# A hybrid trunk layer on one core: KT transposed behind the scores, an opening between the joins, and a merge that begins in the front

## The chip, the cores and the metric

The kernel runs on one core of a Trainium2 chip. The metric is the device time in microseconds, the median over runs. Besides the runs there is one profiled execution of each kernel, from which all rows and durations below come.

## The reference, cut to what matters

One layer: a norm, one wide projection, an RWKV-7 branch (8 heads of 64), a forgetting-attention branch (8 heads), a gated merge of both, an output product, and an MLP. There are 512 tokens and 16 meta tokens ahead of them (T = 528), D_MODEL = 1024, D_FF = 4096, all in float32.

```python
def reference(x, meta, norm_mix, w_in, b_gate, ..., w_out_rw, w_out_fx, w_o, norm_mlp, w_up, w_down):
    h = jnp.concatenate([meta_b, x], axis=1)
    u = rmsnorm(h, norm_mix[l])
    proj = u @ w_in[l]
    feat_rw = proj[..., :C_RW]
    feat_fx = proj[..., C_RW:C_RW + C_FX]
    gates = jax.nn.sigmoid((proj[..., C_RW + C_FX:] + b_gate[l]).astype(jnp.float32))
    y_rw = rwkv7_branch(feat_rw, ...)     # S_t = S_{t-1} (diag(w_t) + a_t^T b_t) + v_t^T k_t ;  y_t = S_t r_t
    y_fx = fox_branch(feat_fx, ...)       # softmax(q k^T * scale + F_q - F_k) v, causal
    merged = gates[..., :D_MODEL] * (y_rw @ w_out_rw[l]) + gates[..., D_MODEL:] * (y_fx @ w_out_fx[l])
    h = h + merged @ w_o[l]
    z = rmsnorm(h, norm_mlp[l])
    h = h + jnp.square(jax.nn.relu(z @ w_up[l])) @ w_down[l]
    return h[:, N_META:]
```

## The kernel before

**Products.** A weight block of 128 x 512 comes by DMA as `wraw`; ScalarE (ACT) casts it to `whi`, VectorE (DVE) subtracts for the low part `wlo`. The activations are split in the same way, and each product is three matmuls: high by high, high by low and low by high (`passes`). The projections write tiles `pj` (L582), 24 matmuls of 264 columns for half of a block of 128 features.

**The front.** Up to 400 us, the order of TensorE (PE) is written out by `Turns`: streams of work, each a generator that yields a function saying when it can go on. The stream of the lowest rank that is ready, by the estimate in `Clock`, issues its next piece. Ranks: 0 the chains, 1 the recurrent part (decay, keys, scores, inverse), 2 attention, 3 its features, 4 group norm and the split of the branch outputs, 8 the projections, which fill what is left. `Clock.read` books every new instruction on its engine with an estimated duration. Only PE is held to this order; the other engines' queues are ordered by the scheduler, with priority for ranks 0 and 1. An instruction waits in its engine's queue until all it reads is there, and what is behind it waits with it.

**PSUM.** Eight banks: four under the tag "sm" (scores, transposes, attention), two "pj" for projections, one "ch" and one "py" for the chain, which the projections borrow when no chain runs. A ring gives a bank back when its reader is done.

**Scores** (`scores`, L951). A pair is two heads. Its nine chunks go in three groups. A group takes two sm banks: `sb` is read by DVE into `Bm` (L965), `sk` by DVE into two halves of `L` (L967). Then the three chunks of `KT` are transposed into a third bank, `pbt` (L971), which ACT copies to `bkT`. `KT` (L924) is made by DVE from `BK` (L922).

**Inverse and chain.** `inverse` joins the halves of a triangular inverse with small matmuls (32 x 32 and 64 x 32 tiles). The chain then goes chunk by chunk: `Rs` (L1111) is the copy that its second matmul needs. L893 is the scan `lc` of a pair's decay. `nm` (L762) is a maximum of attention, `y_rw` (L1095) the chain's output.

**Merge** (L1250 to L1273). For each of eight blocks m and both branches, four k-blocks by three passes go into a bank "sm" (`po`, L1267); DVE multiplies it with the gate `gl` (L1269), a tile that is loaded from DRAM (`gd`, stored by L596), and passed through tanh on ACT (L1262) first. The tiles `gl` lie where tiles of the front lay. ACT has another function table for tanh than for the front's exp and ln, hence a table load there. Then come the output product (L1298, L1329) and the MLP (L1357, L1484).

Of the kernel before, what the change touches and what calls it, by code (L numbers as in the profile page):

```python
# [62 lines left out]
class Clock:  # L63
# [35 lines left out]
    def read(self):  # L99

        new = self.nc.cur_bb.bb.instructions[self.seen:]
        self.seen += len(new)
        for x in new:
            outs = [o.bass_ap for o in x.outs if hasattr(o, "bass_ap")]
            ins = [o.bass_ap for o in x.ins if hasattr(o, "bass_ap")]
            if not outs:
                continue
            for o in outs:
                t = o.tensor
                if hasattr(t, "cap_key") and t.name not in self.free:  # L110
                    ring, n = self.rings.setdefault(str(t.cap_key).rsplit("_", 2)[0], []), t.tag_meta.bufs
                    self.free[t.name] = self.last(ring[-n]) if len(ring) >= n else 0.0
                    ring.append(t.name)
            names = [a.tensor.name for a in ins]
            out = outs[0].tensor.name
            eng = "Pool" if out.startswith("wlo") else str(x.engine).split(".")[-1]

            def cols(a):
                return math.prod(n for _, n in a.ap[1:])
            deps = max([self.w.get(n, 0.0) for n in names] + [self.free.get(out, 0.0)])  # L120
            if eng == "PE":
                n = cols(outs[0])
                rows, width = x.tile_size
                if ins[0].dtype == F32R:
                    cost = n / 2400 + 0.013
                else:
                    cost = n / 600 * max(rows * width / 16384, 1 / 4)
                if self.form != tuple(x.tile_size):
                    self.form = tuple(x.tile_size)
                    cost += 0.1  # L130
                self.pe = end = max(self.pe, deps) + cost
            else:
                size = max([cols(a) for a in outs + (ins if "Reduce" in str(x.opcode) else [])])
                if eng in self.RATE and "DMA" not in str(x.opcode):
                    fixed, per = self.RATE[eng]
                    if eng == "DVE" and (getattr(x, "is_tensor_tensor_scan", False) or any(a.ap[-1][0] > 4 for a in outs + (ins[:1] if "Transpose" in str(x.opcode) else []))):
                        per *= 2
                    end = self.book(eng, max(deps, self.last(out)), fixed + per * size) + fixed + per * size
                else:
                    cost = 0.3 + size * 128 * 4 / 2.0e5  # L140
                    end = self.book("DMA", max(deps, self.last(out)), cost) + cost + 2.0
            for o in outs:
                self.w[o.tensor.name] = max(self.w.get(o.tensor.name, 0.0), end + self.HOP)
            for n in names:
                self.r[n] = max(self.r.get(n, 0.0), end + self.HOP)
# [44 lines left out]
def kernel(ctx, tc, ht, x, win, par, cst, gain, lora, wout, wo, wup, wdn, out, dbg=None):  # L190
# [92 lines left out]
    ps = ctx.enter_context(tc.tile_pool(name="ps", bufs=2, space=PSUM))  # L283
    gates_d = [dr.tile([128, S], F32, name=f"gd{i}") for i in range(16)]
    ys = {}
    quarters = [[wdn[i][256 * c:256 * c + 256] for c in range(8)] for i in range(4)]

    with ExitStack() as st:
# [254 lines left out]
        def convert(job, raws):  # L543
# [9 lines left out]
                w.append((hi, lo))  # L553
            return job, w

        def projections(total):
            fetched, done = None, 0
            while done < total:
                if fetched is None:
                    yield lambda: 0.0 if jobs else math.inf  # L560
                    fetched = fetch(jobs.pop(0))
                cur = convert(*fetched)
                fetched = fetch(jobs.pop(0)) if jobs else None
                while cur is not None:
                    (_, _, _, begin, parts, ev, need), w = cur
                    nxt = convert(*fetched) if fetched else None
                    fetched = fetch(jobs.pop(0)) if jobs else None
                    if need is not None:
                        yield need
                    evac = begin()  # L570
                    for a0, a1 in parts:
                        po = None
                        n = 0
                        for k in range(KB):
                            if k % 2 == 0 or a1 - a0 > 300:
                                yield lambda f=po is None: max(ck.ready(*w[k // 4]), block_bank()[0] if f else 0.0)
                            if po is None:
                                tag = block_bank()[2]
                                po = ppj(tag)[:, :a1 - a0]
                                lent.extend([tag] * (tag != "pj"))  # L580
                            for a, b in passes(wk(w, k), U):
                                mm(po, a, b[:, k, a0:a1], start=n == 0, stop=n == 23)  # L582
                                n += 1
                        evac(po, slice(a0, a1))
                        if tag in lent:
                            lent.remove(tag)
                    ev.done = True
                    done += 1
                    cur = nxt

        def gate_job(i):
            def begin():
# [13 lines left out]
        def two(j, k):  # L606
            ys[4 * j + k] = t = kp.tile([128, 2, S], F32R, name="ys", tag=SLOTS[(4 * j + k) // 2], bufs=2)
            return t[:, 0, :], t[:, 1, :]

        def divided():  # L610
            yield chained[1]
            for k in range(2):
                split(*two(0, k), y_rw[:, k, :])
            for k in range(3):
                yield fox_done[k]
                split(*two(1, k), y_fx[:, k, :])
            yield normalised[1][1]
            for k in range(2, 4):
                split(*two(0, k), y_rw[:, k, :])

        forgot = Event()

# [102 lines left out]
        def attention():  # L725
# [3 lines left out]
            for p in range(4):  # L729
# [67 lines left out]
                def mixed():  # L797
# [10 lines left out]
                    if p < 3:  # L808
                        A.copy(y_fx[:, p, :], py)
                    else:  # L810
                        yield chained[1]
                        split(*two(1, 3), py)

                pes = yield from scored(0)
                for i in range(4):
# [39 lines left out]
        class Pair:  # L855
# [96 lines left out]
            def scores(self):  # L952
# [5 lines left out]
                for c0 in range(0, NCH, 3):  # L958
# [6 lines left out]
                    V.tensor_tensor(Bm[:, c0:c0 + 3, :], sb[:, :3, :], bc(tmask, 1, 3), ALU.mult)  # L965
                    for e, os in enumerate(hss[::-1]):
                        V.tensor_tensor(L[e][os, c0:c0 + 3, :], sk[os, :3, :], bc(tmask[os], 1, 3), ALU.mult)  # L967
                    yield lambda: max(ck.ready(KT) + 1.0, banks(1))
                    pb = psm("pbt").rearrange("p (a b) -> p a b", b=128)
                    for c in range(c0, c0 + 3):  # L970
                        nc.tensor.transpose(pb[:, c - c0, :], KT[:, c, :, :].rearrange("p a b -> p (a b)"), ident)  # L971
# [4 lines left out]
        def inverse(g, Bms, late):  # L976
# [54 lines left out]
            for n, pr_, c in cells:  # L1031
                for e, hs in enumerate(hss):
                    mm(p1[hs, n, :], Tt[qs[2 * e], c, pr_, :], W2[qs[2 * e], n, :], start=True, stop=True)
            for n, pr_, c in cells:
                for q in range(4):
                    mm(p2[qs[q], n, :], W2[qs[q], n, :], Tt[qs[q], c, pr_, half(q)], start=True, stop=True)
# [190 lines left out]
        turns.add(3, fox_features())  # L1227
        turns.add(4, divided())
        turns.add(8, projections(24 + 16))
        for i in range(16):  # L1230
            ask(9, B_GATE + i, gate_job(i), SEQ)
        with tc.manual_schedule(engines={mybir.EngineType.PE}):
# [16 lines left out]

    with ExitStack() as st:  # L1250
        mp = st.enter_context(tc.tile_pool(name="mp", bufs=1))
        ahead = [load_w(wout[0])]
        mhi = mp.tile([128, KB, S], F32R, name="mhi")
        mlo = mp.tile([128, KB, S], F32R, name="mlo")
        table["pin"] = None
        for m in range(KB):
            w = ahead.pop() if ahead else load_w(wout[m])
            pp = []
            for br in range(2):
                g = mp.tile([128, S], F32, name=f"gl{br}", bufs=2)  # L1260
                nc.sync.dma_start(g, gates_d[8 * br + m])
                act(g, g, AF.Tanh, scale=0.5)  # L1262
                po = ppo()
                n = 0
                for k in range(4 * br, 4 * br + 4):
                    for a, b in passes(wk(w, k), (0, 1)):
                        mm(po, a, ys[k][:, b, :], start=n == 0, stop=n == 11)  # L1267
                        n += 1
                V.scalar_tensor_tensor(g, g, 1.0, po, ALU.add, ALU.mult)  # L1269
                pp.append(g)  # L1270
# [20 lines left out]

        pd = [ppo(), ppo(), ppd(), ppd()]
        for b2 in range(4):
            w = load_w(wo[0, b2])
            for i, b1 in [(i, b1) for b1 in range(2) for i in range(4)] if b2 < 3 else [(i, b1) for i in range(4) for b1 in range(2)]:
                k = 2 * b2 + b1
                for n, (a, b) in enumerate(passes(M, w[b1])):
                    mm(pd[i], a[:, k, 128 * i:128 * i + 128], b, start=k == 0 and n == 0, stop=k == 7 and n == 2)  # L1298
# [317 lines left out]
```

## Time and profile before

| | us |
|---|---|
| median of 3 runs | 828.11 (827.68 to 828.64) |
| profiled execution | 826.71 |
| its span | 824.9 |
| PE busy | 808.1 |
| DVE busy | 607.8 |
| ACT busy | 452.5 |
| GpSimd busy | 120.0 |

PE is the engine that is always busy; the granted clock is 0.998 of 2.4 GHz in the mean. Records of PE overlap, so a matmul's cost is taken from the start of one to the start of the next. Stages by PE's lines: the norm up to 31 us, the front to 400, the merge to 445, the output product to 491, the MLP to the end.

### The profile page before, as it was taken

The page shows a single profiled execution, that of the slowest core. Times are in us where ns is not written, and L with a number is a line of the kernel's source. Part 1 is how long each engine was busy: PE and PEld are TensorE (multiplying, and loading weights), DVE is VectorE, ACT ScalarE, POOL GpSimd, SP SyncE. Part 2 cuts the span into 40 slices and gives each one's busy share as a digit, 9 for nine tenths or more (in the row PEclk, how much of TensorE's full clock was granted, in tenths as well). Part 3 has the DMA queues.
Part 4 walks back from the last instruction along what each step waited for, and adds up shares of the span by engine and source line. Part 5 has one row for each costly group of instructions (what it writes and reads, how often), then busy time and mean ns, then how long its engine had stood idle before and what let it go on. Part 6 is the DMA issues. An engine that isn't in the chain of part 4 may idle for free.

```text
span 824.9 us, 15506 instructions
## 1 busy us (share of the span) xinstructions
PE 808.1 (98%) x5886; PEld 667.3 (81%) x5886; DVE 607.8 (74%) x1196; ACT 452.5 (55%) x941; POOL 120.0 (15%) x124
## 2 busy tenths in 40 slices
PE   8999999998999999999999999999999999999998
PEld 6979887876987886778788889888888888888886
DVE  6797985687779855975267655875698678867988
ACT  7767548766575457664366534664445434543452
POOL 1021000010011000000022003100740174017400
PEclk9999999999999999999999999999999999999999
DMA  7222221211211311223687404533742365236532
GB/s 240 75 71 79 69 92 56 79 40 65 79 52 54 128 46 61 90 66 116 218 289 226 159 0 151 176 82 100 225 150 87 115 221 150 77 118 208 156 107 76
DMA packets 51483, 95.88 MB, mean 116 GB/s; under 512 B 5832, under 2 KB 7240, under 8 KB 51408
## 3 DMA queue, kind: packets, MB, share of 16 engines
q1 hardware_dynamic: 47680, 86.37, 33.0%
q0 software_dynamic: 1280, 4.20, 1.7%
q10 hardware_dynamic: 2448, 4.33, 1.5%
q8 instruction: 46, 0.75, 0.4%
q14 instruction: 29, 0.24, 0.1%
HBM read 88.56 MB, written 6.31 MB: 115 GB/s over the span
## 4 chain that ended last, share of the span: by engine, by line
PE 86%; DVE 5%; ACT 5%; issue 2%; DMA 1%; POOL 0%; DVEq 0%; ACTq 0%; SPq 0%
PE pj L582 22%; PE po L1357 21%; PE po L1484 12%; PE pd L1484 5%; PE po L1267 4%; PE po L1329 3%; PE pj L394 1%; PE pd L1298 1%; PE po L1298 1%; PE psc L751 1%; PE py L805 1%; PE psr L964 1%; PE ppt L788 1%; DVE wlo L551 1%; PE pch L1115 1%
## 5 line engine op out<-in xcount | busy, mean ns | idle before, releaser
L582 PE MATMUL pj<-uhi,whi 128*128 128x264 f32 (+1 forms) x480 | 164.3, 342 | 0.0
L582 PE MATMUL pj<-uhi,wlo 128*128 128x264 f32 (+1 forms) x480 | 153.9, 321 | 1.8 <-DVE wlo L551 1.8
L582 PE MATMUL pj<-ulo,whi 128*128 128x264 f32 (+1 forms) x480 | 153.8, 320 | 0.0
L242 DVE TENSOR_TENSOR wlo<-wraw,whi 128x512 fp32r<-128x512 f32 x84 | 81.0, 973 | 36.8 <-ACT whi L242 36.8
L582 PEld LDWEIGHTS pj<-uhi,whi 128*128 128x128 f32 x480 | 90.7, 189 | 12.9 <-issue 4.4
L582 PEld LDWEIGHTS pj<-uhi,wlo 128*128 128x128 f32 x480 | 90.7, 189 | 8.8 <-DVE wlo L551 2.2
L582 PEld LDWEIGHTS pj<-ulo,whi 128*128 128x128 f32 x480 | 91.0, 190 | 6.7 <-issue 1.6
L1357 PE MATMUL po<-zhi,whi 128*128 128x512 f32 (+1 forms) x248 | 94.8, 382 | 0.0
L1357 PE MATMUL po<-zlo,whi 128*128 128x512 f32 (+1 forms) x248 | 94.8, 382 | 0.0
L1357 PE MATMUL po<-zhi,wlo 128*128 128x512 f32 (+1 forms) x248 | 94.8, 382 | 0.0
L242 ACT CAST whi<-wraw 128x512 fp32r<-128x512 f32 x84 | 51.4, 617 | 53.5 <-PE po L1357 20.3
L551 DVE TENSOR_TENSOR wlo<-wraw,whi 128x512 fp32r<-128x512 f32 x78 | 53.8, 699 | 23.5 <-ACT whi L550 22.6
L550 ACT CAST whi<-wraw 128x512 fp32r<-128x512 f32 x78 | 47.7, 617 | 42.4 <-PE pj L582 41.7
L276 ACT CAST whi<-t 128x512 fp32r<-128x512 f32 x64 | 39.9, 624 | 44.6 <-DVE wlo L276 27.2
L1406 POOL TENSOR_TENSOR t<-traw 128x512 f32<-128x512 f32 x24 | 38.4, 1622 | 173.6 <-DMA traw<-in_wdn 173.6
L1484 PE MATMUL po<-wlo,fhi 128*128 128x512 f32 (+1 forms) x164 | 63.4, 387 | 0.2
L1484 PE MATMUL po<-whi,flo 128*128 128x512 f32 (+1 forms) x164 | 62.8, 384 | 0.0
L1484 PE MATMUL po<-whi,fhi 128*128 128x512 f32 (+1 forms) x164 | 62.3, 384 | 0.0
L276 DVE TENSOR_TENSOR wlo<-t,whi 128x512 fp32r<-128x512 f32 x64 | 43.5, 689 | 24.3 <-ACT whi L276 24.0
L1373 ACT CAST fhi<-R 128x768 fp32r<-128x768 f32 (+1 forms) x32 | 30.2, 945 | 49.1 <-DVE R L1380 26.1
L1357 PEld LDWEIGHTS po<-zlo,whi 128*128 128x128 f32 x248 | 46.6, 188 | 9.1
L1357 PEld LDWEIGHTS po<-zhi,wlo 128*128 128x128 f32 x248 | 46.6, 188 | 9.0
(330 smaller groups left out, 1706.4 us busy)
## 6 DMA issues: line engine op xcount, KB each, us to landing
wraw<-in_win SPq DMA_DIRECT2D x84, 256.0 KB, 2.6
wraw<-in_wup SPq DMA_DIRECT2D x60, 256.0 KB, 3.1
wraw<-in_wdn SPq DMA_DIRECT2D x48, 256.0 KB, 2.7
traw<-in_wdn SPq DMA_DIRECT2D x48, 256.0 KB, 3.5
gd<-gt ACTq DMA_DIRECT2D x16, 256.0 KB, 2.2
wraw<-in_wout SPq DMA_DIRECT2D x16, 256.0 KB, 3.9
gl<-gd SPq DMA_DIRECT2D x16, 256.0 KB, 3.8
traw<-in_wdn POOLq DMA_DIRECT2D x16, 256.0 KB, 3.1
```

The lines of the kernel that those rows point to most:

```text
L242: casts.append((A.copy(hi, raw), low.tensor_tensor(lo, raw, hi.bitcast(F32), ALU.subtract)))
L276: return A.copy(hi, x), V.tensor_tensor(lo, x, hi.bitcast(F32), ALU.subtract)
L550: after(A.copy(hi, raw), last["ACT"])
L551: low[0] = V.tensor_tensor(lo, raw, hi.bitcast(F32), ALU.subtract)
L582: mm(po, a, b[:, k, a0:a1], start=n == 0, stop=n == 23)
L1267: mm(po, a, ys[k][:, b, :], start=n == 0, stop=n == 11)
L1298: mm(pd[i], a[:, k, 128 * i:128 * i + 128], b, start=k == 0 and n == 0, stop=k == 7 and n == 2)
L1329: mm(po, a[:, k, 128 * i:128 * i + 128], b[:, k, :], start=n == 0, stop=n == 23)
L1357: mm(po[:, t0:t1], a, b[:, k, t0:t1], start=n == 0, stop=n == 23)
L1373: A.copy(fhi[:, j, a:b], R[:, a:b])
L1406: eng.tensor_tensor(t, sums[c, pair] if c in (T1, T2) else c, d, ALU.add)
L1484: mm(x[i][:, cols], a[:, k, left, 128 * rows:128 * rows + 128], c[:, cols], start=start and k == 0 and n == 0, stop=stop and k == n_pairs ...
```

## The change

- **Estimates.** A split matmul costs as much as its rows' share of 128, a transpose n/1200 instead of n/600 at full width, and a change of tile form 0.18 or 0.14 instead of 0.1.
- **Scores.** The transposes of KT leave the loop over groups and come in a loop of their own behind all three groups, and a margin of 1.0 in their readiness is dropped.
- **Joins.** `inverse` yields once between its second and third loop of small matmuls, so another stream may step in.
- **Merge.** A stream `merging` of rank 8 does the k-blocks 0, 1 and 4 to 7 of the blocks m = 0 (in two pj banks) and m = 1 (in ch and py), once the last projection is issued. The merge adds k = 2 and 3 there and does m = 2 to 7 as before, branch 1 first. The weights of block 0 are loaded ahead of the last gate block, the others one line ahead, into the output product.

```diff
@@ Clock.read
-                if ins[0].dtype == F32R:
-                    cost = n / 2400 + 0.013
+                split = ins[0].dtype == F32R
+                if split:
+                    cost = (n / 2400 + 0.013) * rows / 128
+                elif x.is_transpose:
+                    cost, width = n / 1200, 128
                 else:
                     cost = n / 600 * max(rows * width / 16384, 1 / 4)
-                if self.form != tuple(x.tile_size):
-                    self.form = tuple(x.tile_size)
-                    cost += 0.1
+                if self.form != (rows, width):
+                    self.form = (rows, width)
+                    cost += 0.18 if split else 0.14
@@ projections
+                    if done == total - 1:
+                        begun.append(load_w(wout[0]))
+            projected.done = True
+
+        def merging():
+            yield projected
+            for m in range(2):
+                w = begun.pop() if m == 0 else load_w(wout[m])
+                pos = []
+                for br, ks in ((0, (0, 1)), (1, (4, 5, 6, 7))):
+                    if m:
+                        yield chained[1]
+                    tag = ("pj", ("ch", "py")[br])[m]
+                    yield lambda: max(ck.ready(*w[br]), ck.ring(tag, 1, 1 if m else 2))
+                    po = ppj(tag)
+                    n = 0
+                    for k in ks:
+                        while k not in parted:
+                            yield lambda: math.inf if k not in parted else 0.0
+                        yield lambda: ck.ready(parted[k])
+                        for a, b in passes(wk(w, k), (0, 1)):
+                            mm(po, a, ys[k][:, b, :], start=n == 0, stop=n == 11)
+                            n += 1
+                    pos.append((po, n))
+                under[m] = w, pos
@@ scores
-                    yield lambda: max(ck.ready(KT) + 1.0, banks(1))
+                for c0 in range(0, NCH, 3):
+                    yield lambda: max(ck.ready(KT), banks(1))
                     pb = psm("pbt").rearrange("p (a b) -> p a b", b=128)
@@ inverse
+            at = ck.pe
+            yield lambda: at
@@ merge
-        ahead = [load_w(wout[0])]
+        line = [wout[m] for m in range(2, KB)] + [wo[0, b2] for b2 in range(4)]
+        ahead = []
         for m in range(KB):
-            w = ahead.pop() if ahead else load_w(wout[m])
+            w, pos = under.get(m) or (ahead.pop(0), [])
+            ahead.append(load_w(line.pop(0)))
-            for br in range(2):
+            for br in (1, 0):
-                po = ppo()
-                n = 0
-                for k in range(4 * br, 4 * br + 4):
+                po, n = pos[br] if pos else (ppo(), 0)
+                for k in range(4 * br + n // 3, 4 * br + 4):
...
-            w = load_w(wo[0, b2])
+            w = ahead.pop(0)
+            if line:
+                ahead.append(load_w(line.pop(0)))
```

The stream is added by `turns.add(8, merging())`, and `divided` records in `parted` which branch outputs are split.

**How the order moves.** PE, scores of pair 1, before: projections behind the second group, the transposes of its KT (pbt), and the begin of the third group (psr_1234 and psr_1235).

```order
L582 MATMUL pj_1197<-ulo_100,whi_1050 128x264
L582 MATMUL pj_1197<-uhi_99,wlo_1051 128x264
L582 MATMUL pj_1197<-uhi_99,whi_1050 128x264
L582 MATMUL pj_1197<-ulo_100,whi_1050 128x264
L582 MATMUL pj_1197<-uhi_99,wlo_1051 128x264
L971 MATMUL pbt_1227<-cs_63,KT_1037 128x128 x3
L964 MATMUL psr_1234<-L0_1066,BK_1036 64x128
L964 MATMUL psr_1234<-L1_1067,BK_1036 64x128
L964 MATMUL psr_1235<-L0_1066,BK_1036 64x128
```

After, the third group's end (psr_1199 and psr_1200), with the transposes behind it:

```order
L1002 MATMUL psr_1200<-L1_1067,BK_1024 64x128
L1002 MATMUL psr_1199<-L0_1066,BK_1024 64x128
L1002 MATMUL psr_1199<-L1_1067,BK_1024 64x128
L1002 MATMUL psr_1200<-L0_1066,BK_1024 64x128
L1002 MATMUL psr_1200<-L1_1067,BK_1024 64x128
L1010 MATMUL pbt_1216<-cs_63,KT_1025 128x128 x3
L1010 MATMUL pbt_1223<-cs_63,KT_1025 128x128 x3
L590 MATMUL pj_1146<-uhi_99,whi_1054 128x264
L590 MATMUL pj_1146<-ulo_100,whi_1054 128x264
```

The transposes of two groups stand together, and the third group ahead of all of them.

DVE, pair 1, from KT's first half to the first Bm, before:

```order
L921 SCALAR_TENSOR_TENSOR KT_1037<-okk_864,lc_902 128x9x64
L306 MEMSET tm_1064 128x1
L922 SCALAR_TENSOR_TENSOR BK_1036<-tha_844,KT_1037 128x9x64
L310 SCALAR_TENSOR_TENSOR ov_1062<-pj_1078,pr1_65,tm_1064 128x264
L924 TENSOR_TENSOR KT_1037<-BK_1036,P_904 128x1152
L310 SCALAR_TENSOR_TENSOR ov_1062<-pj_1105,pr1_65,tm_1064 128x264
L551 TENSOR_TENSOR wlo_1133<-wraw_1058,whi_1132 128x512
L551 TENSOR_TENSOR wlo_1137<-wraw_1060,whi_1136 128x512
L306 MEMSET tm_2185 128x1
L965 TENSOR_TENSOR Bm_1077<-psr_1173,cs_63 128x384
```

After:

```order
L959 SCALAR_TENSOR_TENSOR KT_1025<-okk_874,lc_902 128x9x64
L555 TENSOR_TENSOR wlo_1055<-wraw_971,whi_1054 128x512
L960 SCALAR_TENSOR_TENSOR BK_1024<-tha_835,KT_1025 128x9x64
L310 MEMSET tm_1064 128x1
L962 TENSOR_TENSOR KT_1025<-BK_1024,P_904 128x1152
L314 SCALAR_TENSOR_TENSOR ov_1062<-pj_1078,pr1_65,tm_1064 128x264
L555 TENSOR_TENSOR wlo_1133<-wraw_1058,whi_1132 128x512
L314 SCALAR_TENSOR_TENSOR ov_1062<-pj_1105,pr1_65,tm_1064 128x264
L555 TENSOR_TENSOR wlo_1137<-wraw_1060,whi_1136 128x512
L310 MEMSET tm_2162 128x1
L1003 TENSOR_TENSOR Bm_1077<-psr_1159,cs_63 128x384
L1005 TENSOR_TENSOR L0_1066<-psr_1160,cs_63 64x384
```

The weight part wlo_1055 stands between KT's first half and BK now (before, it stood six rows ahead of KT); between BK and Bm there are KT, two shifts ov and two wlo in both.

ACT, start of the merge: casts of wout, the last gate's store (gd15), table load and tanh, before:

```order
L242 CAST whi_5441<-wraw_5439 128x512
L242 CAST whi_5447<-wraw_5445 128x512
L595 ACTIVATE gt_5374<-pj_5349,pr_64 128x512
L596 DMA gd15_95<-gt_5374 128x512
L242 CAST whi_5490<-wraw_5488 128x512
L242 CAST whi_5496<-wraw_5494 128x512
L1262 ACT_TABLE_LOAD
L1262 ACTIVATE gl0_5402<-gl0_5402 128x512
L1262 ACTIVATE gl1_5419<-gl1_5419 128x512
L1262 ACTIVATE gl0_5451<-gl0_5451 128x512
```

After (5411 and 5417 belong to block 1, 5456 and 5462 to block 2):

```order
L245 CAST whi_5411<-wraw_5409 128x512
L245 CAST whi_5417<-wraw_5415 128x512
L628 ACTIVATE gt_5386<-pj_5361,pr_64 128x512
L629 DMA gd15_95<-gt_5386 128x512
L245 CAST whi_5456<-wraw_5454 128x512
L1306 ACT_TABLE_LOAD
L1306 ACTIVATE gl1_5466<-gl1_5466 128x512
L245 CAST whi_5462<-wraw_5460 128x512
L1306 ACTIVATE gl0_5470<-gl0_5470 128x512
L245 CAST whi_5485<-wraw_5483 128x512
```

The cast of the second half of block 2 stands behind the table load and the first tanh; before, both casts of the block in that place stood ahead of them.

## Rows read from the trace of the kernel before

**Rows 1.** Page, part 1: busy us (share of the span) x instructions.
```profile
PE 808.1 (98%) x5886; PEld 667.3 (81%) x5886; DVE 607.8 (74%) x1196; ACT 452.5 (55%) x941; POOL 120.0 (15%) x124
```

**Rows 2.** Waits of PE: us in total, times, longest us.
```profile
PE pbt L971 <- DVE KT L924: 2.1, 2, 1.3
...
PE pj L582 <- DVE wlo L551: 1.8, 1, 1.8
...
PE pch L1115 <- DVE Rs L1111: 1.7, 3, 1.2
...
PE psc L751 <- DVE nm L762: 1.5, 1, 1.5
...
PE po L1267 <- DVE gl L1269: 1.0, 1, 1.0
...
PE py L1143 <- ACT y_rw L1095: 0.6, 1, 0.6
...
PE psr L964 <- DVE Bm L965: 0.4, 1, 0.4
...
PE psr L964 <- DVE BK L922: 0.3, 1, 0.3
```

**Rows 3.** Timeline of PE, pair 1: start, us, what [idle <-releaser].
```profile
84.84 0.89 PE L964 MATMUL psr<-L,BK 64*64 64x128 f32 x24 [0.28 <-DVE BK L922]
...
86.51 0.55 PE L971 MATMUL pbt<-cs,KT 128*128 128x128 f32 x3 [0.78 <-DVE KT L924]
...
86.81 0.37 PE L582 MATMUL pj<-uhi,whi 128*128 128x264 f32 x1
...
88.59 0.87 PE L964 MATMUL psr<-L,BK 64*64 64x128 f32 x20 [0.45 <-DVE Bm L965]
...
91.46 0.39 PE L582 MATMUL pj<-uhi,whi 128*128 128x264 f32 x1
...
91.69 0.28 PE L582 MATMUL pj<-ulo,whi 128*128 128x264 f32 x1
...
91.81 0.28 PE L582 MATMUL pj<-uhi,wlo 128*128 128x264 f32 x1
```

**Rows 4.** Timeline of DVE, pair 1.
```profile
84.03 0.76 DVE L922 SCALAR_TENSOR_TENSOR BK<-tha,KT 128x576 f32<-128x576 f32 x1
...
85.10 1.35 DVE L924 TENSOR_TENSOR KT<-BK,P 128x1152 f32<-128x1152 f32 x1
...
86.37 0.48 DVE L310 SCALAR_TENSOR_TENSOR ov<-pj,pr,tm 128x264 f32<-128x264 f32 x1
...
86.77 1.28 DVE L551 TENSOR_TENSOR wlo<-wraw,whi 128x512 fp32r<-128x512 f32 x2
...
87.98 0.55 DVE L965 TENSOR_TENSOR Bm<-psr,cs 128x384 f32<-128x384 f32 x1
...
88.56 0.56 DVE L967 TENSOR_TENSOR L<-psr,cs 64x384 f32<-64x384 f32 x1
```

**Rows 5.** Timeline of PE, begin of the merge.
```profile
400.06 0.62 PE L1267 MATMUL po<-ys,whi 128*128 128x512 f32 x2
...
400.74 0.62 PE L1267 MATMUL po<-ys,whi 128*128 128x512 f32 x2
```

**Rows 6.** The chain that ended last, begin of the merge: start, us, what.
```profile
401.28 5.43 DMA gd<-gt
...
406.79 2.59 DMA gl<-gd
...
409.43 1.28 ACT L1262
...
410.73 0.64 ACT gl L1262
```

**Rows 7.** Page, part 6: queue, count, KB each, median us to landing.
```profile
gd<-gt ACTq DMA_DIRECT2D x16, 256.0 KB, 2.2
```

**Rows 8.** Page, part 5: busy us, mean ns | idle before.
```profile
L242 ACT CAST whi<-wraw 128x512 fp32r<-128x512 f32 x84 | 51.4, 617 | 53.5 <-PE po L1357 20.3
```

More of the change, by code (lines that the diff above doesn't have):

```diff
@@ L285 @@
     ys = {}
+    under = {}
     quarters = [[wdn[i][256 * c:256 * c + 256] for c in range(8)] for i in range(4)]
@@ L554, in convert @@
             return job, w
+        begun, parted, projected = [], {}, Event()
         def projections(total):
@@ L589, in projections @@
                     cur = nxt
+            projected.done = True
[20 more added lines that the diff above has]
+                under[m] = w, pos
+            return
         def gate_job(i):
@@ L608, in two, with part @@
             return t[:, 0, :], t[:, 1, :]
+        def part(j, k, y):
+            hi, lo = two(j, k)
+            split(hi, lo, y)
+            parted[4 * j + k] = lo
         def divided():
@@ L612, in divided @@
             for k in range(2):
-                split(*two(0, k), y_rw[:, k, :])
+                part(0, k, y_rw[:, k, :])
             for k in range(3):
                 yield fox_done[k]
-                split(*two(1, k), y_fx[:, k, :])
+                part(1, k, y_fx[:, k, :])
             yield normalised[1][1]
             for k in range(2, 4):
-                split(*two(0, k), y_rw[:, k, :])
+                part(0, k, y_rw[:, k, :])
         forgot = Event()
@@ L811, in mixed @@
                         yield chained[1]
-                        split(*two(1, 3), py)
+                        part(1, 3, py)
                 pes = yield from scored(0)
@@ L1229 @@
         turns.add(8, projections(24 + 16))
+        turns.add(8, merging())
         for i in range(16):
```

## The prediction

> **What bounds the kernel now.** I read the page's busy shares first: TensorE (PE) is at work in 98% of the span [rows 1], so nothing that leaves PE's work as it is can give more than its idle time. Both programs issue the same matmuls and transposes with the same operands; only order differs. The price of the change is therefore the sum of the times in which PE stands still, and of the times in which it changes between the full array and a smaller tile form. Next I read PE's waits [rows 2]: the eight rows there that lie in the front and the merge add up to 9.4 us. The wait for the low halves of a weight (wlo, 1.8) is in head pair 0, those for KT (2.1 in two), for BK and for Bm in pairs 1 and 3, that for Rs (longest 1.2) at the start of the first chain, those for nm and y_rw at its end, and that for gl (1.0) at the start of the merge. Last, I read PE and DVE side by side in pair 1 [rows 3, 4], and the chain of waits at the start of the merge [rows 5, 6].
>
> **Prices used.** A projection matmul of 264 columns takes 0.12 us from start to start (91.69 to 91.81), and 0.23 after a score group (91.46 to 91.69), so a return to the full array costs 0.11 [rows 3]; I take the entry at 0.1 too, an estimate from it, and so 0.2 for an excursion. A score group of 12 matmuls (24 rows, two passes each) takes some 0.81 [rows 3]. On DVE, Bm takes 0.55, and the two L behind it end near 1.6 us after Bm's start (88.56 plus two of 0.56 less the overlap of 0.06); KT holds DVE for 1.3, a shift of ov for 0.4, a wlo for 0.6 [rows 4].
>
> **Scores: what moves.** Before, a group of scores took two of the four "sm" banks, and the transposes of KT behind it a third. The wait for KT then stood inside the pair, and while PE sat in it DVE had time to empty the score banks. Now the first two groups take all four banks at once, the third needs the two of the first group back, and the transposes come last. KT leaves the list of waits; the banks, emptied by DVE in order, enter it.
>
> *Pair 1.* Before, PE idles 0.28, 0.78 and 0.45 there; from row starts with the changes of form it is 1.9 [rows 3]. DVE starts Bm 3.95 after BK's start (84.03 to 87.98), because KT, the shifts of ov and two wlo stand between [rows 4], and they still stand there. After: PE starts group 1 at BK's start + 0.81 (84.84); two groups are 1.62, six projection matmuls 0.9 with the changes, so it is ready for group 3 at BK + 3.4. The two banks come free when the second L ends, BK + 5.5. That is a wait of 2.1. Then the second transpose bank waits for group 2's L, some 0.4. One more wlo (1055) now stands between L959 and BK on DVE, so BK is late by up to 0.6 where DVE has no slack. 2.1 + 0.4 + 0.3 (before BK, as now) + 0.4 (two thirds of that wlo) − 1.9 = **+1.3**; bounds −1.0 (banks covered, half of what waits now goes) to +2.0.
>
> *Pair 0.* The 1.8 for wlo goes, since that wlo stands before DVE's long run (KT, BK, L) in the new order; including the return it is 2.0. The same bank wait comes instead: behind BK stand the same five instructions, but L and a wlo come before BK, so PE arrives later against BK. I take 1.7, between 1.3 and 2.1 of pair 1: **−0.3**; bounds −1.9 to +0.5.
>
> *Pair 2.* It has no wait now. Its 54 projection matmuls behind the first group (6.5 us) cover the first two banks; two groups then stand together and the transposes' second bank waits for group 2's L, one Bm-to-L round of 1.6 less PE's group of 0.81 and change: **+0.6**; bounds 0 to +1.3.
>
> *Pair 3.* The longest KT wait, 1.3 [rows 2], goes. By the new order twelve more projection matmuls (1.4) stand ahead of the scores, so of the 2.1 of pair 1 some 0.6 is left: **−0.8**; bounds −1.3 to +0.5.
>
> A rule that speaks against this part: the Trainium skill, "TensorEngine Tiling (Array Packing)", section Performance Considerations, says that tiling speeds TensorE up but not the emptying of PSUM, which may become the limit. The trace agrees: 0.81 us of scores on PE stand against 1.6 us of DVE that empty them [rows 3, 4]. By that rule alone all four pairs would wait, which is the slower rival below.
>
> **Rs.** Now the copy Rs of the chain stands on DVE behind the scan lc of the next pair, and PE waits 1.2 [rows 2]. With the new estimates Rs is issued ahead of that scan. **−1.3** with the change of form; bounds −1.3 to 0. The scan is later by Rs's short copy only, and who needs it has projections beside it.
>
> **End of the first chain.** nm and y_rw cost 1.5 + 0.6 now, 2.6 with the changes. In the new order an L683 and a transpose of P meet in one bank, behind a Ln of ACT, and the last product of the chain stands right behind the copy that it waits for. Waits of about 1.1, 1.0 and 0.8 come to 3.1 with the changes: **+0.5**; bounds ±1.0.
>
> **Opening in the inverse.** A stop is set between two loops of small matmuls where PE does not wait now. Two excursions more, +0.4. Against them, scores in one piece save one excursion per pair, −0.8; the rest of the order nets to −0.1: together **−0.5**; bounds −0.8 to +0.5.
>
> **Merge.** Now the last gate's projection ends at 400.06 (T) [rows 5]; its store takes 5.43 from 401.28, the load of gl 2.59, ACT's table load 1.28 from 409.43, tanh 0.64 from 410.73 [rows 6]. After four banks of 12 products (0.227 each, three in 0.68 [rows 5]) PE needs a bank back at T + 10.9, and waits the 1.0 for gl, 1.2 with the start. After: four more banks were filled before or beside, and gl is needed at T + 21.8; that wait goes, −1.2. But the cast of half 1 of wout[2] now stands on ACT behind table load and tanh, which wait for the same store and load. The new merge takes branch 1, and so half 1, first. The cast ends at T + 9.4 + 1.28 + 0.58 + 0.6 = T + 11.9 (a cast 0.617 [rows 8]), its low half on DVE 0.7 later, PE is there at T + 10.9 (48 products): 1.0 and then 0.35, some 1.4. **+0.2**; bounds −1.2 (the store lands in the median of 2.2 [rows 7], and everything comes 3.2 earlier) to +1.5.
>
> What a page would add: the Trainium skill, "ScalarE: Activation LUTs", section What ACT_TABLE_LOAD costs, gives 1.283 us for the load and 1.38 more for a drain. The trace has the first (1.28) and no second: tanh starts 0.02 after it [rows 6], though ACT was idle before. By the page the cast would be 1.4 later and the sum 1.4 higher.
>
> **Sum.** −0.3 + 1.3 + 0.6 − 0.8 − 1.3 + 0.5 − 0.5 + 0.2 = −0.3. Everything from the output product on is the same. The profiled execution took 826.71 (span 824.9 and 1.8 around it), so 826.4; the median of the runs is 1.4 above it: **827.8**.
>
> **Rivals.**
> *Faster.* The bank waits are covered: casts and so wlo come later in DVE's queue than I put them, Bm and L run up to one ov and wlo pair (1.0 each) earlier in pairs 0, 1 and 3, and the store lands at its median. Pair terms −1.3, 0, 0.2, −1.2, the merge −1.2, Rs −1.3, the rest as above: −4.8, some 823.3. For it: the KT waits are certain to go, and what covers a bank costs nothing. Against: a score group needs twice as long to empty as to fill.
> *Slower.* One mechanism: score banks held by DVE. If each pair pays the full 2.1 for group 3 and 0.7 for the transposes, pairs come to +0.8, +2.0, +1.3 and +0.5 = +4.6 in place of +0.8: 831.6. It decides from the point at which more than three DVE instructions stand between BK and Bm in all four pairs; the rows show that for pair 1 alone.
> *The change does little.* Order on PE alters only locally, the removed waits return as waits elsewhere of equal size: 828.1; it falls into the same case as the forecast.
>
> **How the numbers follow.** Within 0.2% (1.7 us) is no change, about what a measurement of this kernel can tell. Forecast (sum within ±1.7, the little-change rival in it) 0.38; faster rival 0.34; slower 0.28. The likeliest one's own range is 826.4 to 829.8. The whole range goes to both rivals, 823.3 to 831.2, beyond which I leave 2 in 10.
>
> **What would show it.** PE's waits of the changed kernel: no KT; a new row "psr for L" or "psr for Bm" in several pairs of 1 to 2 us each; no Rs row over 0.5; no gl row in the merge, but a row for whi or wlo just after 48 products. If psr rows stay under 1 us in sum, the faster rival is right; if they are over 6 us, the slower. If a wait appears in the second chain or in the inverses, the sum misses a term, and I am wrong for a reason that I did not price.

## The result, and the profile after

The changed kernel takes 831.5 us (median of 4 runs, 831.06 to 833.4) against 827.89 of before on the same chip: a ratio of 1.0049, 95% interval 1.0029 to 1.0069. It is slower by 0.5%. The forecast of 827.8 was wrong and the range, to 831.2, just missed it; the slower rival gave 831.6, which that range left out. The profiled execution has a span of 829.5, 4.6 above before. PE's busy share answers to [rows 1]:

```profile
PE 810.5 (98%) x5886; PEld 667.3 (80%) x5886; DVE 602.6 (73%) x1196; ACT 453.0 (55%) x941; POOL 120.6 (15%) x124
```

The waits of PE in the changed kernel answer to [rows 2] (us in total, times, longest):

```profile
PE psr L1002 <- DVE Bm L1003: 2.9, 2, 1.5
PE psr L1002 <- DVE L L1005: 2.3, 3, 0.8
...
PE pbt L1010 <- DVE L L1005: 1.5, 4, 0.7
...
PE po L1310 <- ACT whi L245: 1.1, 1, 1.1
PE psr L1002 <- DVE tm L310: 0.9, 1, 0.9
PE ppt L824 <- ACT y_fx L1125: 0.8, 1, 0.8
PE psc L789 <- DVE y_rw L1220: 0.7, 1, 0.7
PE ppt L826 <- ACT fsq L723: 0.5, 1, 0.5
PE ppm L824 <- ACT pm L809: 0.4, 1, 0.4
PE py L1184 <- ACT y_rw L1136: 0.4, 1, 0.4
PE pch L1156 <- DVE Rs L1152: 0.3, 1, 0.3
```

Every row for KT, wlo, nm and gl of [rows 2] is gone, and Rs fell from 1.7 to 0.3. In their place stand psr waits of 6.1 us in three rows, pbt waits of 1.5 for L, and a wait of 1.1 for a weight's cast in the merge. The row named for tm is the wait for BK: that memset has no part in the scores and stands right behind BK on DVE. So 5.2 of the 6.1 are waits for banks.

PE in pair 1, against [rows 3] (start, us, what, [idle before <- releaser]):

```profile
86.65 1.54 PE L1002 MATMUL psr<-L,BK 64*64 64x128 f32 x48 [0.88 <-DVE tm L310]
88.12 0.39 PE L590 MATMUL pj<-uhi,whi 128*128 128x264 f32 x1
...
90.53 0.44 PE L1002 MATMUL psr<-L,BK 64*64 64x128 f32 x4 [1.42 <-DVE Bm L1003]
91.77 0.87 PE L1002 MATMUL psr<-L,BK 64*64 64x128 f32 x20 [0.81 <-DVE L L1005]
...
93.39 0.52 PE L1010 MATMUL pbt<-cs,KT 128*128 128x128 f32 x3 [0.27 <-DVE L L1005]
```

DVE in the same stretch, against [rows 4]:

```profile
85.85 0.75 DVE L960 SCALAR_TENSOR_TENSOR BK<-tha,KT 128x576 f32<-128x576 f32 x1
...
86.63 1.36 DVE L962 TENSOR_TENSOR KT<-BK,P 128x1152 f32<-128x1152 f32 x1
87.91 0.49 DVE L314 SCALAR_TENSOR_TENSOR ov<-pj,pr,tm 128x264 f32<-128x264 f32 x1
88.31 0.68 DVE L555 TENSOR_TENSOR wlo<-wraw,whi 128x512 fp32r<-128x512 f32 x1
88.91 0.49 DVE L314 SCALAR_TENSOR_TENSOR ov<-pj,pr,tm 128x264 f32<-128x264 f32 x1
89.31 0.68 DVE L555 TENSOR_TENSOR wlo<-wraw,whi 128x512 fp32r<-128x512 f32 x1
89.92 0.55 DVE L1003 TENSOR_TENSOR Bm<-psr,cs 128x384 f32<-128x384 f32 x1
...
90.50 1.12 DVE L1005 TENSOR_TENSOR L<-psr,cs 64x384 f32<-64x384 f32 x2
```

Read the two side by side. Two groups run together (48 rows, 1.47 us from 86.65 to 88.12), and the projections behind them are done near 89.0. Group 3 needs the bank that Bm empties, and Bm starts on DVE at 89.92, 4.07 after BK's start (3.95 before), behind KT, two ov and two wlo. PE starts at 90.53, does two matmuls, and stands again until 91.77, when both L are done with the second bank. The second transposes at 93.39 wait for the L of group 2. Pair 0 shows the same steps, pairs 2 and 3 the later ones: three psr waits and four pbt waits for L in the four pairs. PE in pair 0, where BK starts on DVE at 49.29:

```profile
52.15 0.40 PE L590 MATMUL pj<-uhi,wlo 128*128 128x512 f32 x1
54.03 0.44 PE L1002 MATMUL psr<-L,BK 64*64 64x128 f32 x4 [1.49 <-DVE Bm L1003]
55.28 0.87 PE L1002 MATMUL psr<-L,BK 64*64 64x128 f32 x20 [0.81 <-DVE L L1005]
...
56.90 0.87 PE L1010 MATMUL pbt<-cs,KT 128*128 128x128 f32 x3 [0.27 <-DVE L L1005]
```

After these waits in pair 0 (PE idle 2.3 us of the 3 between 52.4 and 55.3) the granted clock (column PEclk) is at half, the 1.2 GHz level, for some 3.4 us (stretch, its length, PE busy us with instructions, PEclk, DMA share, GB/s):

```profile
56.00:57.00 1.00, 0.73 (x8) 0.94 0.04 14
57.00:58.00 1.00, 1.00 (x5) 0.50 0.00 0
...
60.00:61.00 1.00, 1.00 (x5) 0.85 0.00 0
```

By row starts (the time from one matmul's start to the next, less what the same matmul takes elsewhere) this costs 1.4 us. Before, the same fall came once too, after the wait for nm at 200; there it cost some 1.6, and the changed kernel has none at that place, so the two nearly cancel:

```profile
204.00:206.00 2.00, 2.00 (x14) 0.50 0.00 0
```

At the start of the merge, ACT (casts, table load, tanh), against [rows 6]:

```profile
407.31 0.62 ACT L245 CAST whi<-wraw 128x512 fp32r<-128x512 f32 x1 [2.87 <-PE pj L618]
412.88 1.28 ACT L1306 ACT_TABLE_LOAD   x1 [4.95 <-DMA gl<-gd]
414.17 0.63 ACT L1306 ACTIVATE gl<-gl 128x512 f32<-128x512 f32 x1
414.71 0.60 ACT L245 CAST whi<-wraw 128x512 fp32r<-128x512 f32 x1
```

PE there, against [rows 5]:

```profile
413.91 0.39 PE L1310 MATMUL pj<-ys,wlo 128*128 128x512 f32 x1
415.36 0.73 PE L1310 MATMUL po<-ys,whi 128*128 128x512 f32 x2 [1.06 <-ACT whi L245]
```

The chain of waits gives the store of the last gate 5.59, and 3.37 to the last of the loads of gl to land, at 414.84. The load that the table load waits for was issued from 410.15 and had landed by 412.88:

```profile
404.47 5.59 DMA gd<-gt
...
411.47 3.37 DMA gl<-gd
```

The cast at 414.71 is the one that PE waits for at 415.36. By the kernel's order its buffer was free at 411.4, when the products of the new stream (L618) end; it stands in the queue behind the table load, which waits for gl until 412.88. The same happens in small at the end of the merge, in the loads of weights into PE (PEld):

```profile
437.75 0.30 PEld L1310 LDWEIGHTS po<-ys,whi 128*128 128x128 f32 x2 [0.41 <-ACT whi L245]
438.48 0.19 PEld L1310 LDWEIGHTS po<-ys,wlo 128*128 128x128 f32 x1 [0.43 <-DVE wlo L245]
```

The cast behind those stood on ACT behind a tanh that waited 1.64 for its gl; with a second place like it at 443, the row starts of PE lose 1.1 us.

### The profile page after: what moved, and what is told of

Its sections match the earlier page's. It is cut to its first block, busy times and chain, and to the rows that moved or that the text cites. A ratio compares the mean times of both kernels' runs of the same rounds, so it can differ in the third digit from the quotient of the medians.

```text
span 829.5 us, 15508 instructions
## 1 busy us (share of the span) xinstructions
PE 810.5 (98%) x5886; PEld 667.3 (80%) x5886; DVE 602.6 (73%) x1196; ACT 453.0 (55%) x941; POOL 120.6 (15%) x124
## 4 chain that ended last, share of the span: by engine, by line
PE 84%; DVE 7%; ACT 4%; DMA 2%; issue 2%; POOL 0%; SPq 0%; DVEq 0%; ACTq 0%
PE pj L590 22%; PE po L1402 21%; PE po L1529 12%; PE pd L1529 5%; PE po L1310 4%; PE po L1374 3%; PE pj L398 1%; PE pd L1343 1%; PE po L1343 1%; PE psc L789 1%; DMA xt<-in_ht 1%; PE py L843 1%; PE ppt L826 1%; DVE L L1005 1%; DVE wlo L555 1%
```

## Experiments

The expectations name theories by letters: A, the third score group waits for banks that DVE holds; B, the new estimates made a worse order; C, casts of weights stand behind the gates on ACT. D, E and F are rivals that are told where they are tested.

All ratios are to runs of the kernel before on the same chip, each with 5 to 12 runs of its own. Where an entry says "order kept", the sequence in which the planner picked its streams was written out as a list, taken from the kernel named, so that no estimate can move anything else. Where the scores are left alone (runs 8, 10, 11), the traces show the front in the same order on every engine as in the kernel that the list came from, up to the last weight parts. In runs 5 and 6 PE differs only in the score rows, and the queues of DVE and ACT shift a little around them:

```diff
+            n = PICKS.pop(0)
+            at = next(i for i, s in enumerate(self.streams) if s[1] == n)
```

**1. Scores as before in the changed kernel, planner free.**

```diff
-                for c0 in range(0, NCH, 3):
-                    yield lambda: max(ck.ready(KT), banks(1))
+                    yield lambda: max(ck.ready(KT) + 1.0, banks(1))
```

> The changed kernel with the scores as before (transposes of KT inside each group, the margin of 1.0 back); estimates, opening and merge stay changed. Theory A (the third score group waits for banks that DVE holds): the waits of psr and pbt for DVE, 7.6 us in the changed kernel, go, and KT waits of about 3 us return: 827 to 828, if the saved Rs waits show too 826. Theory B (the new estimates put weight parts and projections in worse places, the scores only show it): no gain over 1 us, 830.5 to 831.5.

Measured: 1.0090 (1.0078 to 1.0103), slower than the changed kernel. The psr waits for Bm and L did fall to 0.2, as theory A says, but a KT wait of 2.6, a BK wait of 1.4, a whi wait of 2.1 in the merge and several at the end of the first chain came. Neither theory foresaw this: the planner made another order out of the front.

**2. The new place of the transposes in the kernel before, planner free** (the reverse of the diff above).

> The kernel before with only the new place of the transposes; estimates, opening and merge as before. Theory A: 4 us slower than before, 831 to 832, with psr waits for Bm and L of 5 us or more in sum. Theory B: within 1 us of before, since the old estimates keep the old order around the scores.

Measured: 1.0246 (1.0228 to 1.0265), five times what theory A expected. The largest wait is not in the scores:

```profile
PE pyt L1169 <- DVE ysq L1164: 8.3, 1, 8.3
```

The planner put the transposes of a group norm at 179 us, and DVE still had its chain of small steps to do, mixed with keys of pair 2: PE stood 8.3 us. So a run with a free planner does not price a part. The runs below keep the order.

**3. Merge as before in the changed kernel** (no stream `merging`, `for br in range(2)`, `load_w` where it is used).

> The changed kernel with the merge of before (no stream in the front, branch 0 first, weights loaded where they are used); scores, estimates and opening stay changed. Theory C (the merge costs more than it saves, since casts of weights stand behind tanh of the gates on ACT: 2.5 us of PE lost there against 1.2 before): 830.2, 1.3 below the changed kernel. Rival D (the loss lies in the front alone): 831.5, no change.

Measured: 1.0037 (1.0023 to 1.0052), about 1.0 us below the changed kernel's 1.0049, with the gl wait back (1.1). It agrees with C in sign and size, but the intervals overlap, so this run does not show it by itself.

**4. Branch 0 first.**

```diff
-            for br in (1, 0):
+            for br in (0, 1):
```

> The changed kernel, but each block of the merge takes branch 0 first. Theory C: block 2 then begins with the half of its weights that is cast ahead of table load and tanh; the wait of 1.2 plus 0.3 at 414 goes: 830.0. Rival: the same cast is needed 2.7 us later and is late still, or another half is late instead: 831 to 831.5.

Measured: 1.0041 (1.0029 to 1.0053). The whi wait at 414 is gone; a gl wait of 0.3 and two wlo waits of 0.2 each stand later. That is about half of the gain that C names, and inside the intervals' width.

**5. Transposes behind the scores, order of before kept.**

> The kernel before, with its own sequence of streams fixed as a list, so that nothing else can move; only inside the scores the three transposes of KT stand behind the three score groups, in the same slots. Theory A (third score group and second transposes wait for banks that DVE holds, 7.5 us in the changed kernel, against 5.3 us of KT, BK and wlo waits that go or stay): 2 to 4 us slower than before. Rival E (what the scores lose in the changed kernel is only the place that the new estimates gave to weight parts and projections): within 1 us of before.

Measured: 1.0027 (1.0015 to 1.0040), 2.2 us slower: theory A, at the low end of its expectation. Its PE waits:

```profile
PE psr L980 <- DVE Bm L981: 2.6, 3, 1.3
...
PE psr L980 <- DVE BK L938: 1.0, 1, 1.0
PE psr L980 <- DVE L L983: 0.8, 1, 0.8
```

KT is gone, and banks hold PE, with the old estimates and the old order. Rival E falls. The 2.2 is the price with the clock in it: in this profile the granted clock is at half twice, for 3.5 us each from 52.5 and from 93.5, and not behind the wait for nm; in the kernel before it fell once, there. And the wait for gl is 0.3 instead of 1.0, though the merge is untouched, so that wait can differ without any edit to it.

**6. Scores undone, order of the changed kernel kept.**

> The changed kernel, its own sequence of streams fixed as a list, but inside the scores the transposes of KT stand in each group again, in the same slots. Theory A: psr and pbt waits for L and Bm (6.7 us) go, KT waits of about 3 us come back: 2 to 4 us below the changed kernel, 827 to 829. Rival E: within 1 us of the changed kernel.

Measured: 1.0010 (0.9996 to 1.0025), 3.2 us below the changed kernel. Theory A again, from the other side, though not as clean as expected: the waits for L are gone and KT takes 1.1, but 1.7 for Bm and 1.3 for BK stay. No fall of the clock is left in this profile, while the merge's waits are 1.9 against the 1.1 of the changed kernel.

**7. The new estimates alone, planner free** (the first part of the diff).

> The kernel before with the new estimates of TensorE's durations alone. Theory B (estimates nearer to the trace on one engine, with weight parts still booked on another, give a worse order): 3 to 6 us slower than before. Rival: the Rs waits go (2 us) and the rest keeps its level: 1 to 2 us faster.

Measured: 1.0000 (0.9982 to 1.0018). Waits moved, from nm, wlo and gl to BK, Rs and y_fx; without those of the first norm they add up to 8.0 against 9.4, while a second fall of the clock came (from 86.5), and the time is the same. Theory B falls. Of the rival's 1 to 2 us, 1 lies inside the interval. So no cost of the estimates by themselves is seen, to within 1.5 us.

**8. The merge alone, order of before kept** (and the list continued by the new stream).

> The kernel before with its sequence of streams fixed, and the merge of the changed kernel (begun in the front behind the last projection, weights loaded ahead, branch 1 first). Theory C (casts of weights behind the gates' tanh on ACT): 0.5 to 1.5 us slower than before, with a whi wait near 1.2 where before has the gl wait of 1.2, and two of 0.5 at the end of the merge. Rival: the gl wait goes and nothing comes: 1.2 faster.

Measured: 1.0026 (1.0012 to 1.0040), 2.1 us slower, more than C expected. The gl wait is gone; the waits for whi and wlo are 2.4 by this view and 2.9 by row starts, where before has 1.2:

```profile
PE po L1320 <- DVE wlo L258: 1.6, 2, 0.9
...
PE po L1320 <- ACT whi L258: 0.8, 1, 0.8
```

The 0.8 is the cast behind the table load, as C says. The two waits for wlo, at the end of the merge, have another source beside C:

```profile
434.74 1.45 DVE L258 TENSOR_TENSOR wlo<-wraw,whi 128x512 fp32r<-128x512 f32 x1 [0.54 <-ACT whi L258]
...
441.17 1.68 DVE L258 TENSOR_TENSOR wlo<-wraw,whi 128x512 fp32r<-128x512 f32 x1 [0.30 <-ACT whi L258]
```

These two took 1.45 and 1.68 us where a wlo takes 0.69 in the same place of the changed kernel. GpSimd adds two gates at the same time (L1324, 1.30 us from 434.34 and 1.28 from 441.01). The 0.8 and 1.0 that they took longer are about the two waits of 0.74 and 0.88. So the price of the begun merge also depends on what falls beside these parts, and this run's 2.1 is not the changed kernel's merge term.

**9. Low halves of two weight blocks on GpSimd, order of the changed kernel kept.** This takes the four wlo between BK and Bm in pairs 0 and 1 out of DVE's queue; the rest of the front's order stays.

```diff
+        GPS = (4, 8)
...
+            nth[0] += 1
...
-                low[0] = V.tensor_tensor(lo, raw, hi.bitcast(F32), ALU.subtract)
-                after(low[0], last["DVE"])
+                if nth[0] in GPS:
+                    G.tensor_tensor(lo, raw, hi.bitcast(F32), ALU.subtract)
+                else:
+                    low[0] = V.tensor_tensor(lo, raw, hi.bitcast(F32), ALU.subtract)
+                    after(low[0], last["DVE"])
```

> The changed kernel with its sequence of streams fixed; only the low halves of two weight blocks, the four wlo that stand on DVE between BK and the first Bm of pairs 0 and 1 (0.6 us each), are computed on GpSimd. Theory A: Bm and L come 1.2 earlier in both pairs, PE's psr waits fall by 1.2 in each, 2 to 3 us below the changed kernel: 828 to 829. Rival F (something other than DVE's queue holds the banks, or the GpSimd parts come late themselves): no gain, 831.

Measured: 1.0009 (0.9999 to 1.0019), 3.3 us below the changed kernel, somewhat more than expected; rival F falls. DVE in pair 1:

```profile
83.65 0.75 DVE L982 SCALAR_TENSOR_TENSOR BK<-tha,KT 128x576 f32<-128x576 f32 x1
...
86.64 0.55 DVE L1025 TENSOR_TENSOR Bm<-psr,cs 128x384 f32<-128x384 f32 x1
```

and PE:

```profile
87.24 0.44 PE L1024 MATMUL psr<-L,BK 64*64 64x128 f32 x4 [0.33 <-DVE Bm L1025]
88.49 0.87 PE L1024 MATMUL psr<-L,BK 64*64 64x128 f32 x20 [0.81 <-DVE L L1027]
```

Bm starts 2.99 after BK instead of 4.07, and PE's first wait is 0.33 instead of 1.42; the second, for the two L, stays at 0.81. The same in pair 0 takes 1.1 from its wait, and the clock does not fall there:

```profile
57.00:58.00 1.00, 1.00 (x8) 1.00 0.00 0
```

1.1 in each pair and 1.4 of clock are 3.6. Against them the wait for BK in pair 0 grew by 0.4 and those of pair 3 by 0.5, and the merge lost 0.3 less: 3.0, as much as lies between the two spans (829.5 and 826.5). The two L's 0.81 in pairs 0 and 1 did not move: that part is the emptying itself.

**10. Tanh behind the casts, order of the changed kernel kept.**

```diff
-                act(g, g, AF.Tanh, scale=0.5)
+                tanh_ = act(g, g, AF.Tanh, scale=0.5)
+                after(tanh_, casts[-1 if m == 0 else -3][0])
```

> The changed kernel with its sequence fixed; on ACT the tanh of a block's gates must stand behind the weight casts that were issued up to there, for block 0 behind both halves of block 2. Theory C: the whi wait of 1.2 and the wlo wait of 0.3 at 414 go, the two late casts at the end of the merge (1.1 in all) stay or go: 1.4 to 2.5 us below the changed kernel, 829 to 830. Rival: tanh comes too late then and the gl wait is back: no change, 831.

Measured: 1.0042 (1.0025 to 1.0059), some 0.6 below the changed kernel, short of the expectation and inside the intervals. Both waits at 414 are gone, but one of 1.4 for a wlo came, until 443.62. Its cast ends at 441.48; on DVE two low parts of the MLP's weights and the product with a gate stand ahead of it until 442.88. Before that ACT, with the casts behind it, had stood 2.3 us for a gate's load, until 436.56.

**11. Order of before kept, merge begun in the front, tanh behind casts, and a third buffer for each gate tile** (`name=f"gl{br}", bufs=3`).

> The kernel before with its sequence fixed, and the begun merge with tanh behind the casts and three buffers instead of two for each gate tile, so that its load is asked earlier. Theory C: none of the merge's waits is left (2.9 us with the merge as changed, 1.2 before): 1.2 below before, 826.1. Rival: the loads of gates and weights share the queues and one of them is late still: 827 to 829.

Measured: 0.9980 (0.9971 to 0.9990), faster than before, and 1.6 us against 1.2 expected. No po wait is left in PE's waits. Theory C holds: with casts free of the gates, the begun merge is a gain. Of the two mendings the third buffer was not run by itself, and the wlo are at 0.69 here, so that nothing of run 8's second source is left either.

**12. Scores undone, order of the changed kernel kept, merge mended as in 11.**

> The changed kernel's sequence with the transposes of KT inside the groups again, and the merge mended as in the run before. Theories A and C together: 827.5 of the run with the scores undone, less the 2.6 of waits in its merge: 825 to 826, below both kernels. Rival: the waits in the merge are set by DMA and stay: 827.5.

Measured: 0.9981 (0.9970 to 0.9991), 825.23 us, faster than both kernels. PE's waits have no row for po; what the scores still cost is Bm, BK (the row named for tm) and KT:

```profile
PE psr L1018 <- DVE Bm L1019: 1.7, 2, 0.9
...
PE psr L1018 <- DVE tm L326: 1.1, 2, 0.9
PE pbt L1025 <- DVE KT L978: 1.1, 2, 0.6
```

So the two parts, each with the order kept, cost 0.27% and 0.26%, and the estimates nothing that is seen: 0.53% against 0.49% measured for the whole. The intervals are 0.12% and more to either side, so this agreement is loose. Taken from the other end, undoing the scores gives back 0.39% (run 6) and leaves 0.10% for the rest. The spans say it more closely: of the 4.6 us between them, by row starts, 3.2 are lost ahead of the merge and 1.4 in it. The opening in the joins was not run by itself; runs 6 and 12 contain it and are at 1.0010 and 0.9981, so it is not likely to cost much.

## Why the prediction was wrong

**What was right.** That PE's standing still prices the change; that KT, wlo, Rs, nm and gl leave the list; that banks held by DVE enter it; that a cast behind table load and tanh replaces the gl wait, with PE 48 products on. The test written for the slower rival, psr rows over 6 us, came out at 6.1, with 0.9 for BK in it, and its mechanism is what runs 5, 6 and 9 show. I had it as a term, and gave it too little weight. That the rival's 831.6 meets the measured 831.5 is partly luck: it put the merge at +0.2 and no clock in the sum, and did not have pair 3 falling.

**Pair 0, the step that failed.** The prediction said −0.3, since "L and a wlo come before BK, so PE arrives later against BK". PE did not arrive late enough: it waited for BK by 0.2 and was through its next three matmuls 3.1 us after BK's start, as in pair 1. Then it stood 1.65 + 1.07 + 0.43 by row starts, with the 0.2 in all 3.35 where 1.7 was put, against the 2.0 that went: +1.4. On top came the clock at half, +1.4, for which the sum had no term.

**Pair 1.** Predicted +1.3; 4.1 against 2.2 by the same count of before: +1.9. The mechanism and its place are right; sizes were off. Two groups take 1.47, not 1.62, so PE is ready at BK + 3.1 instead of 3.4; both L end at BK + 5.8 instead of 5.5; the wait for BK is 1.04, not 0.7; and before, PE lost 2.2 rather than the 1.9 that I subtracted.

**Pairs 2 and 3.** +1.1 for +0.6, and −0.2 for −0.8. In pair 3 the twelve projections ahead covered less than I took.

**Rs.** −1.6 for −1.3: by row starts 2.5 went and 0.9 came. **End of the first chain.** +1.2 for +0.5, with more waits than priced (a first Ln, a copy y_fx, a transposed pm), but the clock's fall at 203 went with the nm wait, about −1.6. **Opening and forms** cannot be told apart from the rest.

**Merge.** +1.3 for +0.2. The wait at the start was 1.5 by row starts, as worked out (1.4). What was missing is the end: the same queue of casts behind gates, whose loads are late, lost another 1.1 at 437 and 443 (with a third buffer and tanh behind the casts, runs 11 and 12, no such wait is left). I looked at block 2 and not at blocks 6 and 7.

These terms and 0.3 that the start lost before the front come to 5.2, against 4.6 between the two spans; the 0.6 left over is near the −0.5 put on opening and forms, but no run shows that it is theirs. Few of the misses are large; nearly all have the same sign, because I took values between the bounds where DVE's queue, full from BK to Bm, spoke for the upper end.

**The rule on emptying PSUM** that was weighed against the change (the Trainium skill, "TensorEngine Tiling (Array Packing)", Performance Considerations) is what decided in the scores. The trace adds that beside the emptying itself (0.55 and 1.1 us) its place in DVE's queue counts: with 1.1 us of weight parts taken from ahead of it in two pairs, most of the loss is gone, the clock's fall with it. **The drain after a table load** (the Trainium skill, "ScalarE: Activation LUTs", What ACT_TABLE_LOAD costs) does not show here either: tanh starts at 414.17, 1.29 after the load's start, and its 1.38 is not in the sum.

## What to carry to other kernels

Before putting work of the same kind together, count the banks that it fills at once, and read on the engine that empties them what stands ahead of the first emptying: that queue comes on top of the emptying's own time, and here it was the part that could be taken away. Work that only feeds a later stage (weight casts and low halves) must not stand behind an instruction that waits for a DMA, and not ahead of one that frees a bank. Where a planner orders the program, fix its sequence before undoing a part, or the run prices another order.

## What the runs showed that was not expected

A one-place change with a free planner moved the time by 2.5% (run 2), nine times its price with the order kept (run 5).

A wait's length alone does not say here whether the clock falls behind it. The granted clock fell to half for 3.4 us after PE had been idle for 2.3 of 3 us in pair 0, and did not fall there in run 9, where the idle time was 1.1 less. But in pair 1 of the same execution PE stood 2.2 of 3 us (the 1.42 and 0.81 above) and the clock stayed at full; run 3 has the same two waits there (1.40 and 0.81), and its clock was at half for some 7 us, from 91.5 on. The wait of 1.8 for a wlo at 49 left the clock at full in the kernel before, and the same wait in run 5 was followed by a fall. What these executions differ in is not shown. The clock weighs as much as the parts that are priced: of the 12 executions of run 12, the eight with a mean granted clock of 0.998 and more took 824.4 to 826.4 us, the four at 0.993 to 0.995 took 827.2 to 828.2.

Weight parts that began on DVE while GpSimd added two gates took more than twice as long as alone: 1.45 and 1.68 us instead of 0.69 in run 8, and 1.50 from 439.92 in the kernel before, where nothing waited for it. A run without GpSimd there was not made.
